# A scheduled decoder trunk on one core: slots and banks by fixed lists, every group's root as a pair of matmuls, both FFN roots ahead of silu, and the key half by transfer

## The chip, the cores and the metric

The kernel runs on one core of a Trainium2 chip. The metric is device time in microseconds for one execution of the whole program; lower is better. The engines are named as in the profile: PE is TensorE (matmul), PEld its weight loads, DVE VectorE, ACT ScalarE, POOL GpSimd, SP SyncE, which issues the transfers.

## The reference, cut to what matters

All tensors are float32, 1024 positions, width 1024, two layers.

```python
for l in range(DEPTH):                                   # DEPTH = 2
    h = rmsnorm(x, attn_norm[l])
    proj = h @ w_in[l]
    (c_q, c_kv, k_r, g_b, g_c, u_conv, u_pool,
     q_sw, k_sw, v_sw) = jnp.split(proj, pts, axis=-1)
    y_a = mla_attention(c_q, c_kv, k_r, mla_q_norm[l], mla_kv_norm[l], w_uq[l], w_ukv[l], cos, sin)
    y_b = short_gated_conv(g_b, g_c, u_conv, conv_w[l])  # g_b * conv3(g_c * u_conv)
    y_c = multiscale_pool(u_pool, pool_w[l], pool_scale[l])
    y_d = swa_sink_attention(q_sw, k_sw, v_sw, swa_sinks[l], slopes)
    gf = jnp.stack([y_a, y_b, y_c, y_d], axis=2)
    gf = gf * lax.rsqrt(jnp.mean(gf * gf, axis=-1, keepdims=True) + RMS_EPS)
    x = x + (gf.reshape(b, s, D_MIX) * mix_norm[l]) @ w_o[l]
    h2 = rmsnorm(x, ffn_norm[l])
    gate, up = jnp.split(h2 @ w_gate_up[l], 2, axis=-1)
    x = x + (jax.nn.silu(gate) * up) @ w_down[l]
return rmsnorm(x, final_norm)
```

In `mla_attention` the queries are `rmsnorm(c_q, q_norm) @ w_uq` and keys and values `rmsnorm(c_kv, kv_norm) @ w_ukv`; rmsnorm is `x * rsqrt(mean(x*x) + 1e-6) * gain`.

## The kernel before, in words

**Layout and precision.** Everything is feature-major: a tile has 128 features on the partitions and 512 positions, a half of the sequence; `HALVES = (1, 0)` is the order in which the halves t are taken. Each float32 operand of a large matmul is split into a high and a low part in fp32r, by a cast on ACT and a subtraction on DVE (`split`, lines 280 and 283; with a gain, 285 and 286), and `mm3` (line 260) makes a product as three matmuls: high by high, high by low, low by high. A norm is never applied to its input: the products are taken of the raw values, and the root `r` of each position is multiplied into the results (`mul_to`, line 359).

**Roots.** `SumSq.add` squares on ACT and adds up on DVE; `rnorm` sums over the 128 partitions by a matmul with a matrix of ones, so that each partition gets the sum, and then makes `r = (sum/n)^-0.5` with Ln, Exp and Square on ACT (lines 349 to 351) and two operations on DVE (352 and 355). The matmul is one fp32 matmul (line 343), or, where `SumSq` was made with `pair`, two fp32r matmuls of the split sum (line 340). Before, the pair form stands at the FFN's norm, the second layer's first norm, the keys' norm and the groups a (MLA) and b (convolution); groups c (pooling) and d (sliding window) and the queries' norm use the fp32 one.

**Stages of a layer.** First come the products of the input projection, mixed with the sliding-window attention, the convolution, the pooling and then MLA, per head and half; each group is normalised (`group_scale`), then the output projection makes the new x. Gate and up are made block by block of 128 features in a seven-product form: x is combined over pairs of feature blocks (`combine`, lines 1132 to 1153, four combinations, each split) and the weights likewise (`GateUp`, with sums on ACT, DVE and POOL; its splits work on 128x1024). The first few blocks f are "plain": their products start before the root `r2` of their half is there, wait in PSUM (`waiting`), and `plain_gates` and `plain_acts` finish them: gate times r, silu (line 1453), POOL's product by r (line 1454), and on DVE the product with up. Down is also made in seven products, with weight sums on POOL. At the end of a layer ACT loads the table for Ln and Exp again (line 1686), behind the last silu.

**Memory.** SBUF holds 47 places of a pair of tiles [128 x 2 x 512], the "slots" u0 to u46. `Slots.pair` takes the place that has been free longest (a queue). A new tile in a place waits for every reader of the old one. PSUM has 8 banks; which bank a tile gets is worked out by `Order.banks` in four rounds of planning.

**Order.** The program is traced once, and `Order` plans it: it lists what each instruction needs, simulates the five engines with a table of costs, takes ranks from a backward pass (`find`), shifts single rows by the table `MOVES` (engine, row, count, distance), and imposes the order on each engine by dependencies without semaphores. So the order on an engine is fixed by the plan, and each engine waits in that order for what its next instruction needs.

**Keys of the sliding window.** `kk` holds the keys of each of two key groups twice, once on the partitions 0 to 63 and once on 64 to 127, so that both query heads of a group find them. The projection gives one half; the other is copied by ACT (cast) and DVE (line 542, 64x512).

Of the kernel before, what the change touches and what calls it, by code (L numbers as in the profile page):

```python
# [18 lines left out]
P = 128  # L19
# [31 lines left out]

class Slots:
# [24 lines left out]
    def free(self, i):  # L77
        h = self.halves[self.dt[i // 2]]
        if i ^ 1 in h:
            h.remove(i ^ 1)  # L80
            self.places.append(i // 2)
# [3 lines left out]
    def free_pair(self, i):  # L85
        self.places.append(i // 2)
# [25 lines left out]
def trunk_kernel(ctx: ExitStack, tc: tile.TileContext, ins, out, given=None):  # L112
# [185 lines left out]
    class SumSq:  # L298


        def __init__(self, n, pair=False):
            self.n, self.pair = n, pair
# [5 lines left out]
        def add(self, t, f, cols=whole, after=None):  # L308
# [5 lines left out]
            if m == 1:  # L314
# [3 lines left out]
                if self.n == P:  # L318
# [6 lines left out]
            if m == self.n // P - self.held.get((t, cols.start), 0):  # L325
                dve.scalar_tensor_tensor(
                    out=a, in0=q, scalar=e, in1=a, op0=ALU.add, op1=ALU.add
                )
# [5 lines left out]
        def rnorm(self, t, cols=whole, tag="t", final=None):  # L334
# [15 lines left out]
            act.activation(r0, r0, AF.Exp, scale=-0.5)  # L350
# [3 lines left out]
            )  # L354
            dve.scalar_tensor_tensor(out=a, in0=q, scalar=1.5, in1=r0, op0=ALU.add, op1=ALU.mult)
# [15 lines left out]
    ratt = [None, None]  # L371

# [45 lines left out]
    for l in range(L):  # L418
# [54 lines left out]
        if l == 0:  # L473
# [18 lines left out]
            for t in range(2):  # L492
# [14 lines left out]
                ratt[t] = ss.rnorm(t)  # L507
# [26 lines left out]
        for t in range(2):  # L534
            f = tmp()
            mul_to(f, pk[t], r_of(t))
            for g, own, oth in ((0, hd, tl), (1, tl, hd)):
                k1, k2 = R.ap(kk[g][0] + t), R.ap(kk[g][1] + t)
                act.copy(k1[own], f[own])
                act.copy(k1[oth], f[own])  # L540
                dve.tensor_tensor(out=k2[own], in0=f[own], in1=rd(k1[own]), op=ALU.subtract)
                dve.tensor_tensor(out=k2[oth], in0=f[own], in1=rd(k1[own]), op=ALU.subtract)
# [130 lines left out]
        def group_scale(g):  # L673

            sg = SumSq(2 * P, g in "b")
# [20 lines left out]
        def conv(ct):  # L696
# [65 lines left out]
        for ct in range(2):  # L762
# [14 lines left out]
            if ct == 0:  # L777
                lagged(bf, af, 2, tl)
                dve.tensor_copy(bf[hd], af[hd])
                src, dst = bf, af  # L780
            else:
# [3 lines left out]
                dve.tensor_copy(bf[hd], af[hd])  # L785
# [665 lines left out]
        def silu(g, r):  # L1451
            nonlocal last_silu
            last_silu = act.activation(g, g, AF.Silu)  # L1453
            pool.tensor_tensor(out=g, in0=g, in1=r, op=ALU.mult)  # L1454
# [123 lines left out]
        plain_acts()  # L1578
# [4 lines left out]
        r2.append(F.ap(ss2.rnorm(HALVES[1], tag="pv")))  # L1583
        plain(1)
# [151 lines left out]
        for n, (c, m) in enumerate(units):  # L1736
# [43 lines left out]
            elif c == B22:  # L1780
# [4 lines left out]
                if m == 1:  # L1785
                    ratt[0] = ss.rnorm(0, tag="pv")
                if m == NM - 1:
                    ratt[1] = ss.rnorm(1, tag="pv")
# [488 lines left out]
```

## Time and profile before

| | |
|---|---|
| median of 3 runs | 2046.87 us (2046.76 to 2048.48) |
| the profiled execution's own time | 2045.58 us |
| its span in the trace | 2043.8 us |
| PE busy | 2025.6 us (99%), 9422 matmuls |
| DVE busy | 1511.1 us (74%) |
| ACT busy | 994.4 us (49%) |
| POOL busy | 551.7 us (27%) |
| DMA | 302.37 MB, mean 148 GB/s |
| granted TensorE clock | 0.9 or more of full speed in each of 40 slices |

The profile is of one execution, taken by the hardware profiler. A row of the timeline has the start in the span, the length, the engine, the line of the kernel, the operation, out<-in by the names of the tiles, how many instructions the row holds, and in brackets how long the engine was idle before it and what it waited for. Rows that hold several instructions merge neighbours of the same kind. Matmuls overlap, so the cost of one is the distance between starts, not its length. A row of a window has its start and end, its length, the busy time of each engine in it with the count of instructions, the granted clock, the mean share in which the 16 DMA engines were busy, and GB/s.

### The profile page before, as it was taken

The page shows a single profiled execution, that of the slowest core. Times are in us where ns is not written, and L with a number is a line of the kernel's source. Part 1 is how long each engine was busy: PE and PEld are TensorE (multiplying, and loading weights), DVE is VectorE, ACT ScalarE, POOL GpSimd, SP SyncE. Part 2 cuts the span into 40 slices and gives each one's busy share as a digit, 9 for nine tenths or more (in the row PEclk, how much of TensorE's full clock was granted, in tenths as well). Part 3 has the DMA queues.
Part 4 walks back from the last instruction along what each step waited for, and adds up shares of the span by engine and source line. Part 5 has one row for each costly group of instructions (what it writes and reads, how often), then busy time and mean ns, then how long its engine had stood idle before and what let it go on. Part 6 is the DMA issues. An engine that isn't in the chain of part 4 may idle for free.

```text
span 2043.8 us, 26551 instructions
## 1 busy us (share of the span) xinstructions
PE 2025.6 (99%) x9422; PEld 1677.5 (82%) x9422; DVE 1511.1 (74%) x2443; ACT 994.4 (49%) x1743; POOL 551.7 (27%) x420
## 2 busy tenths in 40 slices
PE   9999999999999999999999999999999999999998
PEld 7887888878888888888888888888788888888887
DVE  8789979987666578555657898899876666675555
ACT  7447657753333335444433676668433333354342
POOL 0100000037777772000002000000578667710000
PEclk9999999999999999999999999999999999999999
DMA  5211223335555557766413112242455555487642
GB/s 180 99 67 43 79 84 103 133 125 189 171 186 169 181 183 241 267 208 211 144 45 118 37 42 92 63 150 95 148 183 178 185 173 172 159 304 245 205 165 96
DMA packets 142119, 302.37 MB, mean 148 GB/s; under 512 B 13857, under 2 KB 60961, under 8 KB 141985
## 3 DMA queue, kind: packets, MB, share of 16 engines
q1 hardware_dynamic: 141984, 300.66, 43.9%
q8 instruction: 74, 1.21, 0.2%
q14 instruction: 61, 0.49, 0.1%
HBM read 212.00 MB, written 87.56 MB: 147 GB/s over the span
## 4 chain that ended last, share of the span: by engine, by line
PE 94%; DVE 3%; ACT 1%; issue 1%; DMA 0%; POOL 0%; SPq 0%; DVEq 0%; ACTq 0%
PE ps_mm L260 37%; PE ps_s L260 29%; PE ps_t L260 11%; PE ps_pv L260 8%; PE ps_pv L1044 2%; PE ps_t L1032 1%; PE ps_s L978 1%; PE ps_s L980 1%; PE ps_s L979 1%; PE ps_s L573 1%; PE ps_s L850 1%; PE ps_pv L634 1%; PE ps_t L622 1%; PE ps_t L343 1%; DVE u L286 0%
## 5 line engine op out<-in xcount | busy, mean ns | idle before, releaser
L260 PE MATMUL ps_mm<-u,u 128*128 128x512 f32 (+1 forms) x3378 | 833.3, 391 | 5.2 <-ACT u L280 4.0
L260 PEld LDWEIGHTS ps_mm<-u,u 128*128 128x128 f32 x3378 | 616.8, 188 | 131.6 <-ACT u L280 4.8
L260 PE MATMUL ps_s<-u,u 128*128 128x512 f32 x2670 | 634.4, 389 | 1.6 <-DVE tn L352 1.0
L260 PEld LDWEIGHTS ps_s<-u,u 128*128 128x128 f32 x2670 | 500.6, 188 | 108.2 <-DVE tn L352 1.5
L283 DVE TENSOR_TENSOR u<-u,u 128x1024 fp32r<-128x1024 f32 (+2 forms) x400 | 448.2, 1141 | 175.9 <-ACT u L280 137.8
L280 ACT CAST u<-u 128x1024 fp32r<-128x1024 f32 (+2 forms) x400 | 344.9, 881 | 395.4 <-PE ps_s L260 62.7
L260 PE MATMUL ps_t<-u,u 128*128 128x512 f32 (+1 forms) x1124 | 254.6, 377 | 0.4 <-DVE tn L352 0.4
L260 PEld LDWEIGHTS ps_t<-u,u 128*128 128x128 f32 x1124 | 202.3, 188 | 40.3 <-DVE tn L352 0.8
L1454 POOL TENSOR_TENSOR tp<-tp,u 128x512 f32<-128x512 f32 x80 | 127.6, 1595 | 342.2 <-ACT tp L1453 342.2
L260 PE MATMUL ps_pv<-u,u 128*128 128x512 f32 x744 | 177.4, 389 | 0.0
L260 PEld LDWEIGHTS ps_pv<-u,u 128*128 128x128 f32 x744 | 139.6, 188 | 29.0
L1453 ACT ACTIVATE tp<-tp 128x512 f32<-128x512 f32 x80 | 50.6, 633 | 214.5 <-DVE tp L359 214.3
L1041 POOL MEMSET u<- 128x128 f32 x32 | 6.2, 221 | 467.8 <-PE ps_mm L260 117.1
L749 POOL TENSOR_TENSOR u<-u,u 128x512 f32<-128x512 f32 x4 | 5.4, 1342 | 382.0 <-PE ps_t L622 289.9
L280 ACT CAST u<-ps_t 128x512 fp32r<-128x512 f32 (+3 forms) x132 | 65.2, 503 | 49.9 <-PE ps_t L1032 25.6
L285 ACT ACTIVATE u<-u,par 128x512 fp32r<-128x512 f32 x100 | 70.4, 717 | 28.0 <-DVE u L359 11.3
L283 DVE TENSOR_TENSOR u<-ps_t,u 128x512 fp32r<-128x512 f32 (+3 forms) x132 | 75.9, 580 | 10.6 <-ACT u L280 9.5
L1243 POOL TENSOR_TENSOR u<-u 128x512 f32<-128x512 f32 x38 | 73.3, 1930 | 27.9 <-DVE u L283 27.9
L1532 POOL TENSOR_TENSOR u<-u,u 128x352 f32<-128x352 f32 x64 | 75.9, 1185 | 7.6 <-DMA u<-in_w_dn 4.7
L1532 POOL TENSOR_TENSOR u<-u 128x352 f32<-128x352 f32 x64 | 75.2, 1175 | 8.9 <-DMA u<-in_w_dn 7.9
L286 DVE SCALAR_TENSOR_TENSOR u<-u,par,u 128x512 fp32r<-128x512 f32 x100 | 73.2, 744 | 5.5 <-ACT u L285 5.4
L359 DVE TENSOR_TENSOR tp<-tp,u 128x512 f32<-128x512 f32 x76 | 74.2, 976 | 1.5
(208 smaller groups left out, 2331.3 us busy)
## 6 DMA issues: line engine op xcount, KB each, us to landing
u<-in_w_gu SPq DMA_DIRECT2D x92, 512.0 KB, 3.9
ad<-u SPq DMA_DIRECT2D x154, 256.0 KB, 2.3
u<-ad SPq DMA_DIRECT2D x70, 512.0 KB, 5.0
u<-in_w_dn SPq DMA_DIRECT2D x64, 352.0 KB, 3.5
qd<-u SPq DMA_DIRECT2D x64, 352.0 KB, 2.5
u<-qd SPq DMA_DIRECT2D x32, 512.0 KB, 5.2
u<-in_w_in SPq DMA_DIRECT2D x28, 512.0 KB, 3.5
u<-in_w_dn SPq DMA_DIRECT2D x24, 512.0 KB, 5.4
```

What stands on the lines that cost most here:

```text
L260: pe.matmul(o, w, r, start=start and k == 0 and i == 0, stop=stop and k == n - 1 and i == 2, skip_group_check=again,)
L280: a = act.copy(hi, f)
L283: dve.tensor_tensor(out=lo, in0=f, in1=rd(hi), op=ALU.subtract)
L285: a = act.activation(hi, f, AF.Copy, scale=gain)
L286: dve.scalar_tensor_tensor(out=lo, in0=f, scalar=gain, in1=rd(hi), op0=ALU.mult, op1=ALU.subtract)
L343: pe.matmul(p, ones, a, start=True, stop=final is None)
L359: dve.tensor_tensor(out=o, in0=a, in1=b, op=ALU.mult)
L1044: pe.matmul(py[:, c0:], v_of(j, h), R.ap(s)[:, c0:], start=j == 0 and n == 0, stop=j == nj - 1 and n == 1,)
L1243: pool.tensor_tensor(out=q4, in0=q4, in1=F.ap(self.raw[1] + 1), op=ALU.add)
L1453: last_silu = act.activation(g, g, AF.Silu)
L1454: pool.tensor_tensor(out=g, in0=g, in1=r, op=ALU.mult)
L1532: pool.tensor_tensor(out=o, in0=a, in1=b, op=ALU.add)
```

## The change

It has these parts.

- **Slots by a list.** `Slots.pair` no longer takes the place free longest; the list `SLOTS` names the place of each pair in the order in which the program asks for them.
- **Banks by a list.** `BANKS` names the bank of each PSUM tile; the four rounds of planning are gone, `Order.find` runs once.
- **Order.** The dependencies that the planner reads are reduced to those that no other one implies (`shortest`), and `MOVES` is another table.
- **Pairs.** All group roots and the queries' root use two fp32r matmuls of the split sum instead of one fp32 matmul.
- **Queries and keys not scaled by the first root.** `c_q` and `c_kv` are squared and split as they come out of the projection; so that the norm stays the same, the epsilon of that norm is multiplied by the first norm's mean square (`floors`, a Copy on ACT in `rnorm`, added in `SumSq.add`).
- **Convolution.** The two factors of z are multiplied by r squared (Square on ACT) once, instead of each by r.
- **Pooling.** Two copies move from DVE to ACT.
- **Key half by transfer.** The second copy of the keys is made by transfers from SBUF to SBUF, 16 more in the program, instead of by ACT and DVE.
- **Roots ahead of silu.** `plain_acts` now holds silu and stands behind both halves' roots; the table for silu is loaded once, explicitly, behind the second root's Exp. The gate waits in a slot instead of a temporary, and the result stays in it.

By count, 12 of 14 fp32 sums (`ps_t<-u,ones`) go and 24 fp32r matmuls come on PE; DVE has 16 instructions fewer, ACT 14 more, among them 5 table loads instead of 11; SP has 16 transfers more.

```diff
+SLOTS = (
+    "0123456789abcdefghijklmnopqrstuvwxyzABCDEFGHIJK56789abcde0123yno69abzAc512376yC9HdB8FIae"
...
+BANKS = (
+    "0012345301140100114402422110415311033242424243431421430405400612556471051750141015607664"
...
 class Slots:
-        self.places = deque(range(n))
+        self.places = set(range(n))
+        self.given = iter(SLOTS)
...
     def pair(self, dt):
-        i = self.places.popleft()
+        i = DIGITS.index(next(self.given))
+        self.places.remove(i)
...
     class SumSq:
-        def __init__(self, n, pair=False):
-            self.n, self.pair = n, pair
+        def __init__(self, n, pair=False, floor=None):
+            self.n, self.pair, self.floor = n, pair, floor
...
-                if self.n == P:
+                if self.floor:
+                    dve.scalar_tensor_tensor(
+                        out=a,
+                        in0=F.ap(self.floor[t]),
+                        scalar=float(self.n // P),
+                        in1=a,
+                        op0=ALU.mult,
+                        op1=ALU.add,
+                    )
+                    if self.n == P and self.pair:
+                        self.hl[t] = half_split(a)
+                elif self.n == P:
...
-            act.activation(r0, r0, AF.Exp, scale=-0.5)
+            self.exp = act.activation(r0, r0, AF.Exp, scale=-0.5)
             act.activation(q, r0, AF.Square)
...
+            if floors is not None:
+                floors[t] = F.half()
+                act.activation(F.ap(floors[t]), p, AF.Copy, scale=EPS / n)
...
                 act.copy(k1[own], f[own])
-                act.copy(k1[oth], f[own])
                 dve.tensor_tensor(out=k2[own], in0=f[own], in1=rd(k1[own]), op=ALU.subtract)
-                dve.tensor_tensor(out=k2[oth], in0=f[own], in1=rd(k1[own]), op=ALU.subtract)
+                for k in (k1, k2):
+                    sp.dma_start(rd(k[oth]), rd(k[own]))
...
-            sg = SumSq(2 * P, g in "b")
+            sg = SumSq(2 * P, True)
...
-                mul_to(F.ap(z + t), pp[t], r_of(t))
+                act.activation(F.ap(z + t), r_of(t), AF.Square)
+                mul_to(F.ap(z + t), pp[t], F.ap(z + t))
             yield
             pp = project()
             for t in range(2):
-                f = tmp()
-                mul_to(f, pp[t], r_of(t))
-                mul_to(F.ap(z + t), F.ap(z + t), f)
+                mul_to(F.ap(z + t), pp[t], F.ap(z + t))
...
-                dve.tensor_copy(bf[hd], af[hd])
+                act.copy(bf[hd], af[hd])
...
-        sq_q = SumSq(2 * P)
+        sq_q = SumSq(2 * P, True, floors)
...
-                f = tmp()
-                mul_to(f, pp[t], r_of(t))
-                cq[m][t] = half_split(f, pcol(l, PC_QN + m))
-                sq_q.add(t, f)
+                cq[m][t] = half_split(pp[t], pcol(l, PC_QN + m))
+                sq_q.add(t, pp[t])
...
-        sq_kv = SumSq(P, True)
+        sq_kv = SumSq(P, True, floors)
         pp = project()
         for t in range(2):
+            sq_kv.add(t, pp[t])
             s = F.half()
-            mul_to(F.ap(s), pp[t], r_of(t))
-            sq_kv.add(t, F.ap(s))
+            F.free(floors[t])
             r = sq_kv.rnorm(t)
-            mul_to(F.ap(s), F.ap(s), F.ap(r))
+            mul_to(F.ap(s), pp[t], F.ap(r))
...
         def plain_gates():
             for f, u, pg, pu in waiting:
-                gate = tmp("tp")
-                mul_to(gate, pg, r2[u])
-                silu(gate, r2[u])
-                gates.append((f, u, gate, pu))
+                s = F.half()
+                mul_to(F.ap(s), pg, r2[u])
+                gates.append((f, u, s, pu))
...
         def plain_acts():
-            for f, u, gate, pu in gates:
-                acts[f][u] = F.half()
-                mul_to(F.ap(acts[f][u]), pu, gate)
+            for f, u, s, pu in gates:
+                silu(F.ap(s), r2[u])
+                mul_to(F.ap(s), pu, F.ap(s))
+                acts[f][u] = s
...
             last_silu = act.activation(g, g, AF.Silu)
+            behind(last_silu, gate_table)
...
         r2.append(F.ap(ss2.rnorm(HALVES[0], tag="pv")))
         plain_gates()
         combine(0)
-        plain_acts()
...
         r2.append(F.ap(ss2.rnorm(HALVES[1], tag="pv")))
+        gate_table = act.preload_act_table_set("silu_and_others")
+        behind(gate_table, ss2.exp)
+        plain_acts()
...
 MOVES = (
-    "4,31,1,3 4,32,1,2 4,30,1,3 4,13,1,-2 4,12,1,-6 2,155,1,1 2,107,1,-1 2,159,1,12 4,40,1,3 "
...
+    "4,12,1,1 0,704,1,3 2,244,1,3 2,119,1,9 2,159,1,2 0,625,2,2 2,209,4,-1 2,202,3,1 "
...
-        self.need = [list(d.items()) for d in need]
-        self.feeds = [[] for _ in traced]
-        for k, d in enumerate(self.need):
+        self.need = self.shortest([list(d.items()) for d in need])
+        self.feeds = self.turned(self.need)
...
-def scheduled_kernel(fresh, ins_of, rounds=4):
+def scheduled_kernel(fresh, ins_of):
...
-    for _ in range(rounds):
-        banks = plan.banks(plan.find()[2])
-        nc, traced = trace(banks)
-        plan = Order(traced, nc.dependency_edges)
-        found = plan.find()
-        if best is None or found[0] < best[0]:
-            best = found[0], banks, found[1]
-    return trace(best[1], Order.moved(best[2]))[0]
+    banks = [int(b) for b in BANKS]
+    nc, traced = trace(banks)
+    order = Order(traced, nc.dependency_edges).find()[1]
+    return trace(banks, Order.moved(order))[0]
```

The prediction shows the rows of ACT at the first layer's entry into gate/up and of SP at the start, before and now.

More of the change, by code (lines that the diff above doesn't have):

```diff
@@ L2 @@
 import math
+import string
 from collections import defaultdict, deque
@@ L80, in free @@
             h.remove(i ^ 1)
-            self.places.append(i // 2)
+            self.places.add(i // 2)
         else:
@@ L85, in free_pair @@
     def free_pair(self, i):
-        self.places.append(i // 2)
+        self.places.add(i // 2)
 class View:
@@ L325, in add @@
             if m == self.n // P - self.held.get((t, cols.start), 0):
-                dve.scalar_tensor_tensor(
-                    out=a, in0=q, scalar=e, in1=a, op0=ALU.add, op1=ALU.add
-                )
+                if self.floor:
+                    dve.tensor_tensor(out=a, in0=a, in1=q, op=ALU.add)
+                else:
+                    dve.scalar_tensor_tensor(
+                        out=a, in0=q, scalar=e, in1=a, op0=ALU.add, op1=ALU.add
+                    )
                 if cols == whole and self.pair:
@@ L332, in add, with rnorm @@
                 dve.tensor_tensor(out=a, in0=a, in1=q, op=ALU.add)
-        def rnorm(self, t, cols=whole, tag="t", final=None):
+        def rnorm(self, t, cols=whole, tag="t", final=None, floors=None):
             a, n = F.ap(self.acc[t])[:, cols], self.n
@@ L371, in trunk_kernel @@
     ratt = [None, None]
+    floors = [None, None]
     def enter_load(t, k):
@@ L784, in trunk_kernel @@
                 lagged(bf, af, 8, tl)
-                dve.tensor_copy(bf[hd], af[hd])
+                act.copy(bf[hd], af[hd])
                 src, dst = bf, af
@@ L1785, in trunk_kernel @@
                 if m == 1:
-                    ratt[0] = ss.rnorm(0, tag="pv")
+                    ratt[0] = ss.rnorm(0, tag="pv", floors=None if last else floors)
                 if m == NM - 1:
-                    ratt[1] = ss.rnorm(1, tag="pv")
+                    ratt[1] = ss.rnorm(1, tag="pv", floors=None if last else floors)
         for cols in (slice(0, 256), slice(256, HT)) if last else ():
@@ L1906, in __init__, with turned, shortest @@
                         need[k][p] = True
-        self.need = [list(d.items()) for d in need]
-        self.feeds = [[] for _ in traced]
-        for k, d in enumerate(self.need):
-            for p, sync in d:
-                self.feeds[p].append((k, sync))
+        self.need = self.shortest([list(d.items()) for d in need])
+        self.feeds = self.turned(self.need)
+    @staticmethod
+    def turned(need):
+        feeds = [[] for _ in need]
+        for k, d in enumerate(need):
+            for p, sync in d:
+                feeds[p].append((k, sync))
+        return feeds
+    @classmethod
+    def shortest(cls, need):
+        feeds, left = cls.turned(need), [len(d) for d in need]
+        row = [k for k, d in enumerate(need) if not d]
+        for k in row:
+            for j, _ in feeds[k]:
+                left[j] -= 1
+                if not left[j]:
+                    row.append(j)
+        at = {k: x for x, k in enumerate(row)}
+        before, ended, kept = [0] * len(need), [0] * len(need), [[] for _ in need]
+        for k in row:
+            b = e = 0
+            for p, sync in sorted(need[k], key=lambda x: -at[x[0]]):
+                if (e if sync else b) >> p & 1:
+                    continue
+                kept[k].append((p, sync))
+                b |= before[p] | 1 << p
+                e |= ended[p] | (1 << p if sync else 0)
+            before[k], ended[k] = b, e
+        return kept
     @staticmethod
```

33 lines of the change are left out of this document (29 added, 4 removed), and 107 rows, old and new, of the table MOVES.

## The prediction

> **What bounds the kernel now.** The page comes first: the busy times in its part 1, and in its part 4 the shares of the chain of work that ended last.
>
> ```profile
> PE 2025.6 (99%) x9422; PEld 1677.5 (82%) x9422; DVE 1511.1 (74%) x2443; ACT 994.4 (49%) x1743; POOL 551.7 (27%) x420
> PE 94%; DVE 3%; ACT 1%; issue 1%; DMA 0%; POOL 0%; SPq 0%; DVEq 0%; ACTq 0%
> ```
>
> TensorE works for 2025.6 of 2043.8 us, so 18.2 us is all that any reordering could win; more needs fewer or cheaper matmuls. Where the 18.2 us lie is read from the windows of 50 us (start:end, length, then busy time of PE, PEld, DVE, ACT, POOL with their instructions, granted clock, DMA share, GB/s); the row of 150 to 200 is typical of the windows left out.
>
> ```profile
> 0.00:50.00 50.00, 47.65 (x210) 37.96 (x211) 43.54 (x72) 38.60 (x64) 0.20 (x4) 1.00 0.52 184
> 150.00:200.00 50.00, 50.00 (x222) 39.26 (x221) 47.15 (x88) 40.48 (x77) 0.00 (x0) 1.00 0.16 48
> 400.00:450.00 50.00, 46.96 (x204) 37.72 (x203) 44.06 (x60) 30.43 (x46) 16.26 (x10) 1.00 0.26 83
> 800.00:850.00 50.00, 50.00 (x222) 41.43 (x221) 38.58 (x44) 29.95 (x36) 1.57 (x1) 1.00 0.90 309
> 1400.00:1450.00 50.00, 47.61 (x201) 38.32 (x201) 43.29 (x62) 33.63 (x52) 11.21 (x7) 0.97 0.20 69
> 2000.00:2050.00 50.00, 33.96 (x273) 32.93 (x271) 23.86 (x50) 9.40 (x21) 0.00 (x0) 0.92 0.24 85
> ```
>
> Four places lose time: the start (2.35), the two entries into gate/up at 400 and 1400 (3.04 and 2.39), and the end, with the final norm, which the change leaves as it is. The table of PE's waits names the entries (us in total, times, longest):
>
> ```profile
> PE ps_mm L260 <- ACT u L280: 4.0, 2, 2.0
> PE ps_s L260 <- DVE tn L352: 1.0, 1, 1.0
> PE ps_t L260 <- DVE tn L352: 0.4, 1, 0.4
> ```
>
> The 4.0 us wait for ScalarE's casts of the prepared weights, the rest for the second half's root. One ordinary product costs 0.2267 us: 12 in 2.72 us, by this row of the chain.
>
> ```profile
> 448.01 2.72 PE ps_pv L260 x12
> ```
>
> **Roots as pairs.** A sum over 128 rows is one fp32 matmul with ones (two rows of the trace) or, as a pair, two fp32r matmuls. Before, groups c and d and the queries' root are fp32: 2 halves each, 6 a layer, 12 in all. PE's timeline shows one of each kind:
>
> ```profile
> 180.26 1.02 PE L343 MATMUL ps_t<-u,ones 128*128 128x512 f32 x2
> 180.72 0.80 PE L260 MATMUL ps_mm<-u,u 128*128 128x512 f32 x1
> 181.36 0.39 PE L867 MATMUL ps_t<-u,e_r 128*128 128x512 f32 x1
> 403.89 0.62 PE L340 MATMUL ps_pv<-u,ones_r 128*128 128x512 f32 x2
> 404.35 0.86 PE L260 MATMUL ps_t<-u,u 128*128 128x512 f32 x3
> ```
>
> From 180.26 to 181.36 there are 1.10 us for the fp32 sum and one product, so 0.87 for the sum. The pair takes 403.89 to 404.35, 0.46. PE has no gap at either place, so the 0.41 go straight off the end: 12 x 0.41 = **-4.9 us**. If the product in between had hidden part of it, 0.3 each would be left: -3.6. Each pair costs a half-split more: 6 casts and 6 subtractions a layer, on engines whose cover is weighed below.
>
> **Entry into gate/up, layer 0.** The timeline of ACT, DVE, POOL and PE around it:
>
> ```profile
> 405.77 1.28 ACT L349 ACT_TABLE_LOAD   x1
> 407.06 0.60 ACT L349 ACTIVATE tn<-ps_pv 128x512 f32<-128x512 f32 x1
> 408.19 1.28 ACT L350 ACT_TABLE_LOAD   x1
> 413.07 3.03 PE L260 MATMUL ps_s<-u,u 128*128 128x512 f32 x12 [1.04 <-DVE tn L352]
> 415.46 0.68 DVE L355 SCALAR_TENSOR_TENSOR u<-tn 128x512 f32<-128x512 f32 x1
> 420.99 1.04 ACT L280 CAST u<-u 128x1024 fp32r<-128x1024 f32 x1
> 422.05 1.28 ACT L1453 ACT_TABLE_LOAD   x1
> 423.34 0.63 ACT L1453 ACTIVATE tp<-tp 128x512 f32<-128x512 f32 x1
> 423.88 1.03 ACT L280 CAST u<-u 128x1024 fp32r<-128x1024 f32 x1
> 424.05 1.27 POOL L1454 TENSOR_TENSOR tp<-tp,u 128x512 f32<-128x512 f32 x1 [22.09 <-ACT tp L1453]
> 424.96 1.43 PE L260 MATMUL ps_mm<-u,u 128*128 128x512 f32 x5 [1.98 <-ACT u L280]
> ```
>
> ScalarE loads tables three times here (Ln, Exp, silu), because the first half's silu has thrown out the table of Ln and Exp. PE stands for 1.04 and 1.98, 3.02 us. In the new order both roots come before the first silu. ScalarE after the second root's Ln (ps_pv is the sum, tn a temporary, tp a combination of weights, u a slot), before:
>
> ```order
> L349 ACT_TABLE_LOAD
> L349 ACTIVATE tn<-ps_pv 128x512
> L280 CAST u_4218<-tp 128x512
> L350 ACT_TABLE_LOAD
> L350 ACTIVATE tn<-tn 128x512
> L280 CAST u_4215<-tp 128x512
> ```
>
> and now:
>
> ```order
> L403 ACTIVATE tn<-ps_pv 128x512
> L1198 ACTIVATE te<-u_2098,par 128x512
> L320 CAST u_4172<-tp 128x512
> L404 ACTIVATE tn<-tn 128x512
> L320 CAST u_4226<-tp 128x512
> L1639 ACT_TABLE_LOAD
> ```
>
> Two loads are gone between the sum and Exp, and the third stands behind Exp. Further on, at the casts of the prepared weights (128x1024), before:
>
> ```order
> L280 CAST u_4340<-tp 128x512
> L1143 ACTIVATE te<-u_2086,par 128x512
> L280 CAST u_4403<-u_4401 128x1024
> L1453 ACT_TABLE_LOAD
> L1453 ACTIVATE tp<-tp 128x512
> L280 CAST u_4424<-u_4422 128x1024
> ```
>
> and now:
>
> ```order
> L320 CAST u_4352<-tp 128x512
> L320 CAST u_4414<-u_4412 128x1024
> L320 CAST u_2225<-tp 128x512
> L320 CAST u_4371<-tp 128x512
> L320 CAST u_4435<-u_4433 128x1024
> ```
>
> Load and silu, 422.05 to 423.88, 1.83 us, have left the way to the second cast; two short casts (0.6 each) stand there instead. That alone is 0.6 us. The rest comes from the two loads gone at the root, 2.6 us, and from 7 more products (1.6 us) between root and first prepared weight in the new order. Against it: VectorE, one operation in 0.6 us as from 415.46 on (twice that for 1024 columns), has 33 operations up to the subtractions for those weights, some 21 us by my count of the new order, and PE comes there after 94 products, 21.3 us; VectorE nearly sets the pace. And a new chain: the bank of the first half's up product is freed only after table load, silu, POOL's 1.27 and DVE's product, behind the second root; PE needs it after 51 products, 11.6 us, and the chain comes to some 12 (VectorE's 20 operations ahead of that product). So I leave 1.1 of the 3.0 us standing: **-1.9** (0 to -3.0).
>
> The Trainium skill, page "ScalarE: Activation LUTs", section "What ACT_TABLE_LOAD costs", puts about 1.28 us on a load and about 1.38 on a drain beside it, 2.66 a switch. This trace has 1.28 and the next activation 0.01 us behind it (405.77 + 1.28, 407.06). By the page's price three switches fewer would free 4.1 us more on ScalarE, all 3.0 us would go, and the sum would be 1.1 lower.
>
> **Layer 1.** The same entry, with the clock:
>
> ```profile
> 1416.79 0.73 PE L260 MATMUL ps_t<-u,u 128*128 128x512 f32 x2 [0.39 <-DVE tn L352]
> 1430.91 1.28 ACT L1453 ACT_TABLE_LOAD   x1 [0.54 <-DVE tp L359]
> 1433.82 4.14 PE L260 MATMUL ps_mm<-u,u 128*128 128x512 f32 x10 [2.01 <-ACT u L280]
> 1432.00:1438.00 6.00, 4.18 (x11) 3.31 (x12) 4.51 (x8) 2.80 (x5) 1.27 (x1) 0.72 0.15 57
> ```
>
> Waits of 2.4; and behind the 2.01 the granted clock is 0.72 and ten products take 4.14 us instead of 2.27: 1.9 more. The cast waited for load and silu (2.3 us with the 0.54 ahead), which is more than the wait. Of 4.3 us I leave 0.5 for VectorE: **-3.8** (0 to -4.3).
>
> **The start.** SyncE's first issues (u a slot, par the parameters), before:
>
> ```order
> L389 DMA u_116<-in_w_in 128x512
> L479 DMA par<-in_params 128x86
> L375 DMA u_116<-in_xT 128x512
> L389 DMA u_120<-in_w_in 128x512
> L375 DMA u_120<-in_xT 128x512
> ```
>
> and now:
>
> ```order
> L433 DMA u_116<-in_xT 128x512
> L537 DMA par<-in_params 128x86
> L447 DMA u_116<-in_w_in 128x512
> L433 DMA u_120<-in_xT 128x512
> L447 DMA u_120<-in_w_in 128x512
> ```
>
> The first product needs the first and third of them either way; the second weight is now fifth instead of fourth.
>
> ```profile
> 2.12 0.43 SPq L389 DMA_DIRECT2D u<-in_w_in  x1
> 2.59 1.86 SPq L375 DMA_DIRECT2D u<-in_xT  x4
> 7.00 0.62 ACT L280 CAST u<-u 128x512 fp32r<-128x512 f32 x1 [0.65 <-DMA u<-in_w_in]
> 7.67 0.50 PE L260 MATMUL ps_s<-u,u 128*128 128x512 f32 x1 [0.51 <-ACT u L280]
> ```
>
> One issue later is 2.59 - 2.12 = 0.47, and PE already waits for that cast: **+0.5** (-0.1 to +0.7).
>
> **What costs nothing.** The key halves' copies go from ScalarE and VectorE to 16 more transfers.
>
> ```profile
> L542 DVE TENSOR_TENSOR u<-te,u 64x512 fp32r<-64x512 f32 x8 | 5.5, 686 | 0.1
> u<-u SPq DMA_DIRECT2D x8, 128.0 KB, 2.3
> u<-in_w_dn SPq DMA_DIRECT2D x24, 512.0 KB, 5.4
> ```
>
> A transfer of this kind lands in 2.3 us and is read at least 5 us later. It is queued on SyncE ahead of loads of later input weights, at a DMA share of 0.16 (150 to 200), so nobody waits for those. VectorE gives back four operations of 0.69 a layer there, and the scaling of queries and keys by the first root goes: about 8 operations a layer fewer in all, against the 6 subtractions of the pairs, which are counted in that. In the attention VectorE is busy for 47.15 of 50 us while PE stands at 50.00, so the cover is 2.85 us a window, and it becomes thicker. Square instead of a second product by the root, copies moved to ScalarE (40.48 of 50) and silu in slots instead of temporaries lie under the same cover. Without it a layer's twelve extra operations would be at most 7.9 us.
>
> **Sum.** -4.9 - 1.9 - 3.8 + 0.5 = -10.1. The profiled execution took 2045.58 us (span 2043.8) and becomes 2035.5; it lies 1.3 below the median, so the median becomes 2046.87 - 10.1 = **2036.8 us**. About 0.2%, 4.1 us, is what a measurement of this kernel can tell from no change.
>
> **Rivals.** *The stall only re-forms (0.23).* VectorE or the bank behind silu comes as late as ScalarE did before; then pairs and start alone count: -4.9 + 0.5 = -4.4, 2042.5. For it: VectorE at 44.06 and 43.29 of 50 in both windows, its checkpoints level with PE's. Against it: ScalarE is the releaser of 4.0 of the 5.4 us.
>
> *The clock falls anyway (0.12).* At 424.96 a wait of 1.98 us brought no lower clock, at 1433.82 one of 2.01 did: the fall may not hang on the wait, and then the 1.9 us stay: 2038.7. The Trainium skill, page "TensorE: Matmul & The Clock Gate", asks for no idle gap over about 3 us and lets the clock drop after an idle window of about 3.4; by that rule a 2.01 us wait is no cause either, and the rule speaks for this rival. The one trace with one fall cannot settle it.
>
> *Fixed slots hold loads back (0.09), slower.* Which slot a load gets is now written in a list, and a load waits until that very slot is free, where before it took the one free longest. Where gate/up turns into down, the DMA share is 0.90 at 309 GB/s (800 to 850), and a load of 512 KB lands in 5.4 us: one that starts when it is needed costs that. Two bare ones a layer are 21.6 us, less 10.1 is +11.5: 2058.4. It decides from two bare loads in all (10.8). Against it: PE is at 50.00 there, and the list is one order of places for the same number of pairs.
>
> **Chances.** Forecast 0.56, re-formed stall 0.23, clock 0.12, slots 0.09. Half of the re-formed cases would stay above 2042.8 (within 0.2%), and a little of the forecast: faster 0.78, same 0.13, slower 0.09. The range: downwards all entry waits gone and the start at -0.1 (-4.9 - 3.0 - 4.3 - 0.1 = -12.3, 2034.6), with 0.1 us on each of the 12 sums, 2033.4; upwards the re-formed stall with pairs at -3.6, 2043.8. So 2033 to 2044, with only the slots outside.
>
> **What would show it.** Right: no fp32 sums but those of the first and the last norm, and at both entries PE busy for over 48.5 of 50, granted clock 1.00 in both, one table load behind the second Exp. Wrong: a wait of over 1 us on DVE or on a bank at the entries (re-formed stall); a clock under 0.9 without a wait ahead of it (clock); waits of PE for DMA between 700 and 900 us (slots); or group roots that don't shorten the stretch around 180 us by some 0.8 us for each pair of halves.

## The result, and the profile after

The changed kernel takes 2036.68 us (median of 6 runs, 2034.24 to 2038.35) against 2047.48 us (2046.76 to 2048.48, 6 runs): a ratio of 0.9947, 95% interval 0.9934 to 0.996, 10.8 us less. The profiled execution of the changed kernel is the slowest of its six, 2038.35 us with a span of 2036.6 us; its start, below, shows why. First the busy times and the chain:

```profile
PE 2022.5 (99%) x9422; PEld 1679.2 (82%) x9422; DVE 1509.9 (74%) x2427; ACT 995.7 (49%) x1757; POOL 558.6 (27%) x420
PE 98%; DVE 1%; DMA 0%; ACT 0%; SPq 0%; issue 0%; DVEq 0%; ACTq 0%
```

PE is 98% of the chain instead of 94. The windows of the changed kernel show where:

```profile
0.00:50.00 50.00, 45.70 (x190) 37.16 (x191) 38.31 (x64) 37.37 (x62) 0.20 (x4) 0.93 0.63 208
150.00:200.00 50.00, 50.00 (x233) 40.73 (x232) 48.75 (x92) 42.42 (x83) 0.00 (x0) 1.00 0.14 43
400.00:450.00 50.00, 50.00 (x221) 41.02 (x220) 48.95 (x67) 30.30 (x47) 16.69 (x11) 1.00 0.34 107
800.00:850.00 50.00, 50.00 (x222) 41.39 (x222) 36.38 (x44) 28.13 (x35) 1.30 (x1) 1.00 0.89 312
1400.00:1450.00 50.00, 50.00 (x221) 40.85 (x220) 47.73 (x69) 31.87 (x52) 15.53 (x8) 1.00 0.26 86
```

Both entries into gate/up are at 50.00, clock 1.00: all of their loss is gone, not most of it. PE doesn't wait there at all, although VectorE is now busy for 48.95 of 50 us instead of 44.06. The turn from gate/up to down (800 to 850) is as it was, so no load stands bare. And the start has become worse, 45.70 instead of 47.65. The waits of PE over half a microsecond:

```profile
PE ps_s L300 <- ACT u L320: 2.5, 1, 2.5
PE ps_pv L534 <- DVE ones L174: 1.1, 1, 1.1
PE ps_mm L300 <- ACT u L320: 0.7, 1, 0.7
PE ps_s L401 <- ACT tn L400: 0.6, 1, 0.6
```

Three of the four are in the start. The timeline has the transfers' issues, ScalarE's casts of the two weight halves and PE behind them:

```profile
1.65 0.42 SPq L447 DMA_DIRECT2D u<-in_w_in  x1
2.59 0.43 SPq L447 DMA_DIRECT2D u<-in_w_in  x1
5.82 0.62 ACT L320 CAST u<-u 128x512 fp32r<-128x512 f32 x1 [1.36 <-DMA u<-in_w_in]
9.09 0.62 ACT L320 CAST u<-u 128x512 fp32r<-128x512 f32 x1 [1.92 <-DMA u<-in_w_in]
9.76 0.80 PE L300 MATMUL ps_s<-u,u 128*128 128x512 f32 x1 [2.54 <-ACT u L320]
```

The second weight half is issued 0.47 us later than before, as predicted, but is read 2.1 us later (9.09 against 7.00). ScalarE at the first entry, after the second root's Ln:

```profile
405.57 0.58 ACT L403 ACTIVATE tn<-ps_pv 128x512 f32<-128x512 f32 x1
407.42 0.63 ACT L404 ACTIVATE tn<-tn 128x512 f32<-128x512 f32 x1
408.57 1.28 ACT L1639 ACT_TABLE_LOAD   x1
410.39 0.62 ACT L1508 ACTIVATE u<-u 128x512 f32<-128x512 f32 x1
```

One load of 1.28, behind Exp, as the order said. The time came out 0.1 us from the forecast 2036.8, and part of that is luck: the gain is 10.8 instead of 10.1 us, and the median of before, with more runs, has risen by 0.6. Two terms of the sum were off by 1 to 2 us on opposite sides. The experiments price the three terms and the key half; the other parts of the change were not tested one by one.

### The profile page after: what moved, and what is told of

It reads as the page before. It is cut to its first block, busy times and chain, and to the rows that moved or that the text cites. A ratio compares the mean times of both kernels' runs of the same rounds, so it can differ in the third digit from the quotient of the medians.

```text
span 2036.6 us, 26611 instructions
## 1 busy us (share of the span) xinstructions
PE 2022.5 (99%) x9422; PEld 1679.2 (82%) x9422; DVE 1509.9 (74%) x2427; ACT 995.7 (49%) x1757; POOL 558.6 (27%) x420
## 4 chain that ended last, share of the span: by engine, by line
PE 98%; DVE 1%; DMA 0%; ACT 0%; SPq 0%; issue 0%; DVEq 0%; ACTq 0%
PE ps_mm L300 38%; PE ps_s L300 30%; PE ps_t L300 12%; PE ps_pv L300 8%; PE ps_pv L1099 2%; PE ps_t L1087 2%; PE ps_s L1033 1%; PE ps_s L1035 1%; PE ps_s L1034 1%; PE ps_s L631 1%; PE ps_pv L692 1%; PE ps_t L680 1%; PE ps_t L394 1%; PE ps_s L905 1%; DMA u<-in_w_in 0%; PE ps_pv L394 0%
## 5 line engine op out<-in xcount | busy, mean ns | idle before, releaser
L323 DVE TENSOR_TENSOR u<-u,u 128x1024 fp32r<-128x1024 f32 (+2 forms) x412 | 458.7, 1132 | 215.0 <-ACT u L320 174.6
L320 ACT CAST u<-u 128x1024 fp32r<-128x1024 f32 (+2 forms) x412 | 351.6, 873 | 417.0 <-PE ps_s L300 73.0
L1510 POOL TENSOR_TENSOR tp<-tp,u 128x512 f32<-128x512 f32 x76 | 116.5, 1533 | 165.6 <-ACT tp L1508 162.8
L1588 POOL TENSOR_TENSOR u<-u,u 128x352 f32<-128x352 f32 x64 | 84.8, 1326 | 2.7
L325 ACT ACTIVATE u<-u,par 128x512 fp32r<-128x512 f32 x100 | 69.9, 716 | 28.7 <-DVE u L1236 11.6
L1298 POOL TENSOR_TENSOR u<-u 128x512 f32<-128x512 f32 x38 | 63.6, 1674 | 43.5 <-DVE u L323 43.5
L375 ACT ACTIVATE tn<-u 128x512 f32<-128x512 f32 (+1 forms) x91 | 52.7, 595 | 43.2 <-DVE u L1781 39.6
```

The costliest lines, as they stand in the source:

```text
L320: a = act.copy(hi, f)
L323: dve.tensor_tensor(out=lo, in0=f, in1=rd(hi), op=ALU.subtract)
L325: a = act.activation(hi, f, AF.Copy, scale=gain)
L375: act.activation(q, f, AF.Square)
L1298: pool.tensor_tensor(out=q4, in0=q4, in1=F.ap(self.raw[1] + 1), op=ALU.add)
L1588: pool.tensor_tensor(out=o, in0=a, in1=b, op=ALU.add)
```

## The experiments

In all but the last four the order, slots and banks are those of the kernel that is edited: it is planned as it stands, and then single instructions are taken out, put in or shifted in the finished order (in the diffs, EDIT is set once the plan stands). So nothing else moves in the order. Each comparison is with runs made on the same chip, but for the steps between the last four runs and the changed kernel.

**The changed kernel again.** No edit.

> The changed kernel once more, to see how far its start differs from run to run. Theory A (the new order of the first transfers is late by itself): PE again waits 2 us or more for the cast of the second weight half, its transfer lands at 8.5 to 9.1 us, the median is 2035.5 to 2038. Theory B (the late landing of 9.06 us was chance): it lands near 7.6 us, the wait is about 1 us, the median is within 1 us of 2036.7 all the same.

Median 2035.81 us (2035.2 to 2036.08); a third time, beside the later group:

> The changed kernel beside the next two, for their comparison: 2035 to 2038 us, the second weight half landing anywhere from 7.6 to 9.1 us.

2035.18 us (2034.25 to 2038.16). In the two traces the second half lands at 7.59 and 7.91 us instead of 9.06, and PE waits 1.5 and 1.1 us for it. So part of the 2.54 us was chance. That PE waits there at all was not: it does in each of the three traces.

**The first five transfers as before.** Five entries at the end of the table of moves put the weight first on SyncE and on ScalarE.

```diff
 MOVES = (
...
+    "4,2,1,-2 4,1,1,1 4,4,1,-1 1,2,1,-1 1,4,1,-1 1,5,1,-1 "
 )
```

> The changed kernel with the first five transfers, and ScalarE's first operations, in the order of before. Theory A: the second weight half lands at 7 us again, PE's first waits are 0.5, 0.3 and 0.5 us, the clock of the first 50 us goes back to 1.00, and the median falls by 3 to 5 us to 2032 to 2034. Theory B: no change beyond the scatter of the start, 2035.5 to 2037.5.

2034.42 us (2033.86 to 2035.48), 1.4 less than the changed kernel beside it, and the lowest time of all. Its first window and PE's first products:

```profile
0.00:50.00 50.00, 48.13 (x211) 38.35 (x211) 41.76 (x70) 39.25 (x66) 0.21 (x4) 1.00 0.62 208
6.50 0.49 PE L300 MATMUL ps_mm<-u,u 128*128 128x512 f32 x1 [0.52 <-ACT u L325]
7.29 0.50 PE L300 MATMUL ps_mm<-u,u 128*128 128x512 f32 x1 [0.29 <-DVE u L326]
7.62 0.40 PE L300 MATMUL ps_s<-u,u 128*128 128x512 f32 x1
```

The wait for the second half is gone, and the clock is 1.00. Theory A holds in its direction, with a smaller price than the 3 to 5 us that it named: 1.4, a median between the ranges of the two theories, and one of the five times lies in the other kernel's range.

A matmul further on tells what the start cost in each trace: the first sum of a group, which has the same place in PE's order in all of these runs.

| trace | second half lands | clock falls to 0.50 | first group sum starts |
|---|---|---|---|
| first five transfers as before | 6.73 us | no | 148.49 us |
| changed kernel, third time | 7.91 us | no | 149.18 us |
| silu between the roots (below) | 7.89 us | no | 149.18 us |
| changed kernel again | 7.59 us | 8.55 to 11.96 us | 150.05 us |
| VectorE given more (below) | 7.89 us | 8.69 to 12.10 us | 150.40 us |
| changed kernel, first profile | 9.06 us | 8.23 to 15.06 us | 152.51 us |

Where the clock holds, the changed order is 0.7 us behind the old one; where it falls in the start, 1.6 to 4.0. And the start is nearly all of the difference between the first profile and the third: 3.3 of the 3.4 us between their spans (2036.6 and 2033.2).

**The kernel before with the changed start.** The same moves, the other way round.

```diff
 MOVES = (
...
+    "4,2,1,-2 4,1,1,1 4,4,1,-1 1,1,1,1 "
 )
```

> The kernel before with its first five transfers, and ScalarE's first two operations, in the order of the changed kernel (x, parameters, weight, x, weight). Theory (the order itself is late): the second weight half lands at 7.6 us or later instead of 7.0, +0.5 to +3 us against before. Rival (chance): within 0.5 us of before.

2047.48 us against 2046.41, ratio 1.0006 (0.9997 to 1.0015): the direction of the theory, but the interval takes in no change. In the trace the second half lands at 7.54 instead of 6.97 us, the granted clock is 0.50 from 8.33 to 11.74, which it isn't in the trace of before, and PE comes to its first sum with ones (line 343) at 20.84 instead of 19.12 us. The trace gave something else, at the second layer's entry, which this edit doesn't touch:

```profile
1435.39 2.56 PE L260 MATMUL ps_mm<-u,u 128*128 128x512 f32 x10 [1.98 <-ACT u L280]
```

The same ten products as in the trace of before, behind a wait of 1.98 instead of 2.01 us, take 2.56 instead of 4.14: here the clock did not fall, which hides the start's 1.7 us in this execution (span 2043.8, as before).

**The sums as fp32 again.** The splits stay; the first of the pair becomes one fp32 matmul, the second is left out, for c, d and the queries.

```diff
                 for i, h in enumerate(self.hl.pop(t)):
+                    if EDIT[0] and self.whole:
+                        if i == 0:
+                            pe.matmul(p, ones, a, start=True, stop=True)
+                    else:
...
```

> The changed kernel with the sums of groups c and d and of the queries as one fp32 matmul again; the half-splits stay and are not used. If a sum costs PE 0.87 us against 0.46: 12 x 0.41 = +4.9, 2041.6 us. Rival: the fp32 sum hides part of itself behind its neighbour, 0.3 each, +3.6, 2040.3. Rival: the pairs bring nothing (the sum is covered by other waits): under +1.5.

2040.47 us (2038.05 to 2040.8), 4.7 more than the changed kernel beside it: 0.39 a sum. That is the forecast's 0.41 within the scatter, with no hidden part. In the groups of PE the twelve sums are back (24 rows of 594 ns):

```profile
L401 PE MATMUL ps_t<-u,ones 128*128 128x512 f32 x24 | 12.3, 594 | 0.0
L403 PE MATMUL ps_t<-u,ones_r 128*128 128x512 f32 x24 | 9.0, 402 | 0.0
```

**Silu between the roots again.** The first half's gate product goes directly behind the first root, its silu ahead of the second root's Ln, and the explicit table load goes, so that tables are loaded where needed.

```diff
-        gate_table = act.preload_act_table_set("silu_and_others")
-        behind(gate_table, ss2.exp)
...
+    for silu, ln in MARK["silu"]:
+        ks.remove(place[silu])
+        ks.insert(ks.index(place[ln]), place[silu])
...
+    for gate, root in MARK["gate"]:
+        ks.remove(place[gate])
+        ks.insert(ks.index(place[root]) + 1, place[gate])
```

> The changed kernel with the first half's silu (and the gate product ahead of it) between the two FFN roots again, and tables loaded where they are needed: three loads more per layer, 3.8 us of ScalarE. Theory A (the loads on ScalarE's way made the waits): PE waits 2 to 4 us at each entry into gate/up, with or without a lower clock behind it, +4 to +8 us, 2041 to 2045 us. Rival (the new order of the products and slots made the entries smooth, whatever ScalarE loads): under +1.5, 2036 to 2038 us.

2043.40 us (2041.46 to 2044.3), 7.6 more. The timeline of ACT, DVE and PE at the first entry shows how a table load reaches PE:

```profile
403.01 1.28 ACT L1515 ACT_TABLE_LOAD   x1
404.96 1.28 ACT L408 ACT_TABLE_LOAD   x1
407.49 0.69 DVE L1192 SCALAR_TENSOR_TENSOR tp<-tp,te 128x512 f32<-128x512 f32 x1 [1.94 <-ACT te L1203]
407.98 1.28 ACT L409 ACT_TABLE_LOAD   x1
410.45 1.29 DVE L328 TENSOR_TENSOR u<-tp,u 128x512 fp32r<-128x512 f32 x2 [2.27 <-ACT u L325]
413.00 4.62 PE L305 MATMUL ps_t<-u,u 128*128 128x512 f32 x12 [3.40 <-DVE u L1322]
```

ScalarE's loads make the casts of the combinations late; VectorE, whose subtractions wait for those casts, stands idle for 4.2 us; its reads of PSUM, queued behind, free the banks late; PE waits 3.40 us for one. Twelve products then take 4.46 us (413.00 to the next at 417.46) instead of 2.72. The other wait, in layer 1, is 1.80 us, and no lower clock follows it. Theory A holds. The rival falls: with the same lists of slots and banks, and an order that differs in these two instructions and the table loads alone, the waits are there. The edit prices the early silu together with its loads: in layer 1 ScalarE also stood for 1.96 us, until the gate product came, before that silu.

**VectorE given more work at each entry.** The last operation of the first half's root is done five times.

```diff
             dve.scalar_tensor_tensor(out=a, in0=q, scalar=1.5, in1=r0, op0=ALU.add, op1=ALU.mult)
+            for _ in range(4 if EDIT[0] and again else 0):
+                m = dve.scalar_tensor_tensor(out=a, in0=q, scalar=1.5, in1=r0, op0=ALU.add, op1=ALU.mult)
```

> The changed kernel with the last VectorE operation of the first half's FFN root done five times instead of once (it writes the same values), 4 x 0.6 = 2.4 us more on VectorE at each entry into gate/up. Theory C (the prediction's: VectorE nearly sets PE's pace there, with 0 to 1.2 us to spare): PE waits 1.2 to 2.4 us at each entry, +2.4 to +4.8 us. Rival (VectorE has work ahead of PE's need by more than 2 us): PE has no wait there, under +1 us.

2042.39 us (2040.34 to 2044.22), 7.2 more. The four repeats took more than the 2.4 us of the forecast; VectorE at the first entry:

```profile
400.33 0.68 DVE L417 SCALAR_TENSOR_TENSOR u<-tn 128x512 f32<-128x512 f32 x1
401.05 2.87 DVE L419 SCALAR_TENSOR_TENSOR u<-tn 128x512 f32<-128x512 f32 x4
403.84 0.68 DVE L328 TENSOR_TENSOR u<-tp,u 128x512 fp32r<-128x512 f32 x1
```

The next operation starts 3.51 us after the original one (403.84 - 400.33); in the changed kernel's third trace it is 0.60 (398.96 to 399.56). So VectorE got 2.9 us more, and as much in layer 1 (1409.47 to 1412.97). PE's waits:

```profile
PE ps_t L305 <- DVE u L424: 2.6, 1, 2.6
PE ps_s L305 <- DVE u L424: 1.8, 2, 1.0
...
PE ps_t L305 <- DVE u L1325: 0.3, 1, 0.3
```

The 1.8 and 0.3 lie in layer 0, some 2.1 of the 2.9 us; the 2.6 in layer 1, with a lower clock behind it again:

```profile
1425.21 4.59 PE L305 MATMUL ps_t<-u,u 128*128 128x512 f32 x12 [2.56 <-DVE u L424]
1424.00:1430.00 6.00, 4.79 (x14) 3.86 (x15) 6.00 (x10) 5.50 (x9) 0.00 (x0) 0.72 0.14 44
```

So VectorE has about 0.8 us to spare in layer 0 and 0.3 in layer 1, on the way from the root to PE. It is almost level with PE, and without the repeats PE waits for nothing. Theory C holds for what there is to spare (0 to 1.2 us); the time went above its 4.8 us because of the clock, and because the repeats were longer than it had them.

**The key half by copies again.**

```diff
-                for k in (k1, k2):
-                    sp.dma_start(rd(k[oth]), rd(k[own]))
+                act.copy(k1[oth], f[own])
+                dve.tensor_tensor(out=k2[oth], in0=f[own], in1=rd(k1[own]), op=ALU.subtract)
```

> The changed kernel with the second half of the sliding window's keys copied by ScalarE and VectorE again (8 casts and 8 subtractions of 64x512 in the program) instead of by 16 transfers. Theory (the step costs nothing either way, PE is covered there): within 1 us of the changed kernel beside it. Rival (VectorE is at 47 to 49 of 50 us in that stretch, so its 8 x 0.69 us come through in part): +1.5 to +5.5 us. Rival (the transfers hold up the start of the sliding window): -1 us or more.

2036.03 us (2035.79 to 2038.11) against 2035.18 (2034.25 to 2038.16): 0.85, with ranges that overlap. Its trace has two small waits that the changed kernel hasn't, both in the sliding window's start:

```profile
PE ps_t L617 <- DVE u L622: 0.4, 1, 0.4
PE ps_s L641 <- DVE u L622: 0.2, 1, 0.2
```

By these medians the transfers gain at most that much. The theory (within 1 us) stands.

**Both programs without their lists.** The changed program planned as the kernel before is (places by the queue, banks in four rounds), without moves; and the kernel before without moves.

```diff
-    return trace(best[1], Order.moved(best[2]))[0]
+    return trace(best[1], best[2])[0]
```

> The program of the changed kernel planned as the kernel before is (place free longest, banks worked out in four rounds) and with no table of moves. Theory P (the parts of the program carry the gain): against the kernel before without its table of moves, the next run, it is 8 to 12 us faster. Theory L (the fixed lists carry it): the two differ by less than 4 us.

> The kernel before without its table of moves, for comparison with the run above. Its entries into gate/up should wait as long as before's or longer: 2047 to 2065 us.

2081.37 us (2079.37 to 2085.96) and 2065.92 us (2065.18 to 2070.88). Both theories were wrong: without lists the changed program is 15 us slower. The kernel before lies 0.9 us above its own forecast; PE is busy for 46.97 and 48.51 of 50 us at its two entries. The windows of the changed program without lists:

```profile
150.00:200.00 50.00, 45.42 (x198) 35.78 (x197) 41.56 (x77) 35.76 (x68) 0.00 (x0) 0.93 0.15 45
400.00:450.00 50.00, 50.00 (x221) 41.05 (x220) 46.45 (x70) 33.77 (x56) 11.91 (x7) 1.00 0.21 72
1150.00:1200.00 50.00, 45.59 (x221) 36.92 (x220) 46.91 (x128) 36.21 (x89) 0.00 (x0) 0.93 0.11 38
1400.00:1450.00 50.00, 50.00 (x221) 41.12 (x220) 50.00 (x77) 39.32 (x63) 1.38 (x1) 1.00 0.36 134
```

The entries (400 and 1400) are clean without any list, so they don't need the lists. A plan can still spoil them: with the list of slots alone, the run further down, PE is busy for 48.81 us at the first. The loss here is in the attention, above all in one wait for a bank:

```profile
PE ps_t L678 <- DVE tn L404: 6.1, 2, 3.1
PE ps_mm L298 <- ACT u L240: 4.9, 2, 2.4
```

L678 is the sliding window's transposes, L404 the first VectorE operation of a root, which reads that root's sum: the transposes' bank is still held by the sum of a group's root. Behind each of the two waits of 3.1 us the granted clock is 0.50 for 6.83 us (from 164.63 and from 1192.04). Each program was planned once, so how much of the 15 us is the chance of one plan is open.

**The lists one by one.** The changed kernel without moves, then also with the banks worked out in four rounds.

```diff
-    return trace(banks, Order.moved(order))[0]
+    return trace(banks, order)[0]
```

> The changed kernel with its lists of slots and banks but without its table of moves. If the moves carry the cover of the attention stages: 2060 to 2085 us, with PE's waits at 90, 160 and 218 us as in the run without any list (2081). If slots and banks carry it: 2036 to 2050 us.

> The changed kernel with its list of slots, the banks worked out in four rounds as before, and no table of moves. If slots or banks matter without the moves, it lies clearly between the run without any list (2081 us) and the one with both; if not, all three are within 5 us of each other.

2043.02 us (2041.2 to 2044.15) with slots and banks, 2053.20 us (2050.68 to 2055.72) with slots alone. From no list to all, added in this order: 2081.4 - 28.2 (slots) - 10.2 (banks) - 7.5 (moves) = 2035.5, the middle of the two later medians of the changed kernel. These runs come from different chips, on which the kernel before took 2045.8 to 2046.8, and a step holds for this order of adding. Both forecasts hold: slots and banks carry the cover, and slots alone lie clearly between. The moves of the kernel before were worth 20 (2065.92 to some 2046).

## Why the prediction was right or wrong, point by point

- **Pairs, -4.9.** Right: 4.7 measured, and no sum hides behind its neighbour.
- **Entries, -1.9 and -3.8.** The mechanism was right, the size too small. The trace of before lost 7.3 us there (3.0, 2.4 and 1.9 by the clock), the changed kernel loses nothing, and the early silu with its loads costs 7.6 in the changed order; the forecast was 5.7. The terms that failed are "so I leave 1.1 of the 3.0 us standing", and the 0.5 of layer 1. The counts behind them were near (VectorE 21 us, PE 21.3; 0.3 to 0.8 us to spare by the repeats), but where the two are almost level nothing is lost: PE waits for none of it. Of 2.9 us more on VectorE, 2.1 and 2.6 come through. The 12 us of the bank behind silu against PE's 11.6 gave no wait either. I had also left out one link: ScalarE's loads can cost PE its time by starving VectorE. The experiment shows it in full; in the trace of before VectorE waits 0.58 and 1.15 us for ScalarE's casts behind the second root's two loads, though PE's own 1.98 us there is a wait for a cast. VectorE is busy for 25.25 of 30 us at the first entry before and 29.82 after, by the two windows below, of before and of the changed kernel's third run.

```profile
400.00:430.00 30.00, 26.96 (x116) 21.17 (x115) 25.25 (x39) 21.85 (x34) 3.23 (x2) 1.00 0.20 66
```

```profile
400.00:430.00 30.00, 30.00 (x133) 24.41 (x132) 29.82 (x43) 21.62 (x35) 4.08 (x3) 1.00 0.30 97
```

- **Start, +0.5 (-0.1 to +0.7).** Too small: 1.4 by the experiment, and 4.0 in the first profile. Two steps failed. "One issue later is 0.47" takes a landing for the issue plus a constant: in seven traces of the changed kernel and its variants with this order the same transfer, issued at 2.59 or 2.60, landed at 7.59, 7.64, 7.89, 7.89, 7.91, 8.59 and 9.06 us; why single ones land 1 us late or more is open. And the term had no clock in it. Where the clock held, the cost was 0.7, the upper end of my bounds; it is the clock's fall, behind waits of PE of 1.5 us and more there, that made it 1.6 to 4.0. In the kernel before, the new order costs 1.1, not clear of no change.
- **What costs nothing.** Right for the key half (at most 0.85). But "it becomes thicker" is wrong for the cover: VectorE is busy for 48.75 instead of 47.15 of the 50 us from 150 to 200, so the cover is 1.25 instead of 2.85 us, and only just enough (PE 50.00). Nor was it a property of the program alone: without the lists the changed program waits in the attention and loses 15 us to the old one. The lists' share was not a term of my sum, and could not be read from the trace of before. The other edits under the cover were not tested singly.
- **The sum.** 4.7 + 7.6 - 1.4 = 10.9 by the experiments, 10.8 by the median (11.0 and 11.6 in the two repeats): -10.1 was nearly right because the entries' error of 1.9 and the start's of 0.9 partly cancelled, which is luck. That the prices add up to 10.9 doesn't prove each of them: they were taken one at a time in the changed order, where the early silu brings back other waits (3.40 and 1.80) than before had.
- **The rivals.** The stall did not re-form (no wait at the entries); but it is only 0.3 to 0.8 us away. The clock did not fall by itself: in the changed kernel it is 1.00 at both entries, and wherever it fell in these runs PE had stood idle just ahead (below). But the rival's doubt was in part right: the same wait need not bring a fall. The slots held no load back: DMA 0.89 at 312 GB/s at the turn, PE at 50.00; on the contrary, the list of slots took 28 us off the program without lists.

## What to carry to other kernels

A load or a slow operation on an engine with half its time free can still set the end, through the engine that it feeds: look at who is starved next to it, not at its share of busy time. Two engines that are level need lose nothing, as here, with 0.3 to 0.8 us to spare; what there is to spare can be measured by repeating an instruction until it shows, if the length of the repeats is read from the trace too. An edit's price belongs to an order: the same edits were worth -11 us with the lists and +15 without, by one plan each.

## What the runs showed of the hardware

TensorE's clock falls after much shorter waits than I had weighed, and not by the wait's length alone. Behind single waits of 1.50, 1.72, 1.74, 2.01, 2.54, 2.56, 3.07 and 3.40 us, and behind two in a row (1.58 and 0.70, 1.33 and 0.72, 1.22 and 1.17, 0.89 and 0.40), products ran at half speed, 0.43 instead of 0.23 us each, for 3.41 us, at a price of 1.6 to 1.9 us, or, behind 2.54 and 3.07, for 6.83. Behind another 1.50, 1.80, 1.95, twice 1.98 and twice 2.45 us they did not. The kernel before without moves and the changed program without lists, each at a wait of 2.32 us, differ: PE's timelines of the first and of the second.

```profile
421.64 4.61 PE L260 MATMUL ps_s<-u,u 128*128 128x512 f32 x12 [2.32 <-DVE tn L352]
```

```profile
721.45 3.03 PE L298 MATMUL ps_s<-u,u 128*128 128x512 f32 x12 [2.32 <-ACT tn L1374]
```

The times at which the clock changes tell most of why. In each of the 14 traces all its changes lie whole multiples of 3.413 us apart, to 0.01 us, whatever PE did in between: in that of before it rises at 3.97, falls at 1434.15, 419 such steps later, and rises at 1437.57, one more. What goes with a fall is how long PE is idle within one step. The steps at the two waits of 2.32 us, with the step behind each (kernel before without moves, then changed program without lists):

```profile
418.36:421.77 3.41, 1.09 (x6) 0.58 (x5) 2.80 (x5) 3.36 (x7) 0.00 (x0) 1.00 0.10 36
421.77:425.19 3.42, 3.42 (x9) 2.65 (x10) 3.42 (x7) 0.00 (x0) 0.00 (x0) 0.50 0.42 153
```

```profile
717.59:721.00 3.41, 1.54 (x7) 0.94 (x5) 0.58 (x1) 1.66 (x3) 0.00 (x1) 1.00 0.38 104
721.00:724.42 3.42, 2.97 (x13) 2.46 (x14) 2.16 (x2) 1.83 (x3) 3.42 (x2) 1.00 0.44 129
```

The first wait lies whole in one step, idle for 2.32 of 3.41 us, and the clock falls at its end. The second is divided, 1.87 in one step and 0.45 in the next, and the clock holds. So it is with the second layer's entry: in the trace of before the 2.01 us lie whole in the step from 1430.74 to 1434.15; in the other trace the 1.98 are divided, 1.69 and 0.29. Over all 14 traces the clock fell behind every step in which PE was idle for 1.88 us or more, and behind none with less than 1.44; between, both happened, and why is open. So a wait of some 1.5 to 2.5 us costs such a fall or doesn't, by where it lies on the steps, and the second layer of the kernel before lost 1.9 us to the clock in one trace and nothing in another. The Trainium skill, page "TensorE: Matmul & The Clock Gate", section "What's actually happening", has the clock drop after at least one idle window of about 3.4 us, and the window running freely, not reset when a kernel starts. The steps of 3.41 us agree with such a window. That a whole idle window is needed doesn't agree: 2.01 us of one were enough.
